# Two row maps for a subtract-mean-and-square kernel: runs of neighbouring partitions 64 KiB or 128 KiB apart

## The chip, the cores and the metric

The kernel runs on one core of one Trainium2 chip; nothing was launched on the other cores. Times are device microseconds (us) of a whole execution; the profile's span is shorter by some 1.8 us. The runs quoted here are in the fast state, except for four kernels that were looked at once each, whose state is unknown; the profiles report a granted clock of 1.000, and TensorE does no work. "Before" and "after" are the two kernels of the change.

HBM is the chip's main memory, SBUF the core's own memory of 128 partitions, and a DMA is a transfer between the two, shared out over 16 DMA engines. DVE, ACT, POOL and SP are the vector, scalar, GpSimd and sync engines; here SP issues the DMAs. A run is what one partition takes in one gapless piece of HBM, and the pitch is the distance between the starts of neighbouring partitions' runs. The trace records each transfer as packets, one for each run here (80 of the 720 in the two profiles are tiny ones of 4 bytes beside the data); sixteen packets started together, one on each engine, are called a batch. A transfer lands when its completion is seen.

## The reference, cut to what matters

```
x: (1024, 4096) float32, random normal; axis = -1
mean = np.mean(x, axis=axis, keepdims=True)
return ((x - mean) ** 2).astype(np.float32)
```

16.78 MB come in and 16.78 MB go out. Each row of 16 KiB needs its own mean and nothing from any other row, so which partition holds which row is free, as long as the output uses the same map as the input.

## The kernel before

Two tiles of 8.39 MB each lie in SBUF; a partition holds four rows of a tile (`Q = 4`), 64 KiB in one run of HBM. Tile 1 is loaded by two DMAs, a head of 512 columns and the rest; tile 2 by one; each tile is stored by one. All five go through one queue.

```python
Q = 4
HEAD = 512
H = D * 9 // 16                      # 2304 columns of row 2 on ACT, 1792 on DVE
ntiles = B // (P * Q)                # 2
x_t = x.rearrange("(n p q) d -> n p (q d)", p=P, q=Q)
out_t = out.rearrange("(n p q) d -> n p (q d)", p=P, q=Q)
# ... pools: one buffer per tile, so no load waits for a store ...
for i in range(ntiles):
    x_tile = io.tile([P, Q * D], F32)
    cuts = [0, HEAD, Q * D] if i == 0 else [0, Q * D]
    for lo, hi in zip(cuts, cuts[1:]):
        nc.sync.dma_start(out=x_tile[:, lo:hi], in_=x_t[i][:, lo:hi])
    tiles.append(x_tile)
# ... mean_on_act, mean_on_dve, square_on_act: one instruction or two on a row ...
for i in range(ntiles):
    row = [tiles[i][:, q * D:(q + 1) * D] for q in range(Q)]
    m3 = mean_on_act(row[3])
    m0 = mean_on_dve(row[0])
    square_on_act(row[3], m3)
    m1 = mean_on_dve(row[1])
    square_on_act(row[0], m0)
    m2 = mean_on_dve(row[2])
    square_on_act(row[1], m1)
    square_on_act(row[2][:, :H], m2)
    back = row[2][:, H:]
    nc.vector.tensor_scalar_add(out=back, in0=back, scalar1=m2)
    nc.vector.tensor_mul(out=back, in0=back, in1=back)
    nc.sync.dma_start(out=out_t[i], in_=tiles[i])
```

Of the kernel before, what the change touches and what calls it, by code (L numbers as in the profile page):

```python
# [2 lines left out]

os.environ.setdefault("NEURON_RT_ULTRASERVER_MODE", "4")

# [4 lines left out]

F32 = mybir.dt.float32
ACT = mybir.ActivationFunctionType


@with_exitstack
def kernel(
    ctx: ExitStack,
    tc: tile.TileContext,
    x: bass.AP,
    axis: bass.AP,  # L20
    out: bass.AP,
):




    nc = tc.nc

    B, D = x.shape
    P = nc.NUM_PARTITIONS  # L30
    Q = 4
    HEAD = 512
    H = D * 9 // 16
    assert B % (P * Q) == 0
    ntiles = B // (P * Q)
    inv_d = 1.0 / float(D)

    x_t = x.rearrange("(n p q) d -> n p (q d)", p=P, q=Q)
    out_t = out.rearrange("(n p q) d -> n p (q d)", p=P, q=Q)

    io = ctx.enter_context(tc.tile_pool(name="io", bufs=ntiles))
    scratch = ctx.enter_context(tc.tile_pool(name="scratch", bufs=1))
    stats = ctx.enter_context(tc.tile_pool(name="stats", bufs=2 * ntiles * Q))

    tiles = []
# [7 lines that stand above are left out]
    inorder = tc.keep_in_program_order  # L53

    def mean_on_act(row):
        copy = scratch.tile([P, D], F32)
        neg_mean = stats.tile([P, 1], F32)
        nc.scalar.activation(  # L58
            out=copy, in_=row, func=ACT.Identity, scale=-inv_d, accum_out=neg_mean
        )  # L60
        return neg_mean

    def mean_on_dve(row):
        neg_sum = stats.tile([P, 1], F32)
        neg_mean = stats.tile([P, 1], F32)
        inorder(nc.vector.reduce_sum(  # L66
            out=neg_sum, in_=row, axis=mybir.AxisListType.X, negate=True
        ))
        inorder(nc.vector.tensor_scalar_mul(out=neg_mean, in0=neg_sum, scalar1=inv_d))  # L69
        return neg_mean  # L70

    def square_on_act(part, neg_mean):
        inorder(nc.scalar.activation(  # L73
            out=part, in_=part, func=ACT.Square, bias=neg_mean, scale=1.0
# [18 lines that stand above are left out]
# [1 line left out]
_INS = ['x', 'axis']  # L94
_OUTS = [((1024, 4096), 'float32')]

_NUMBERS = {'axis': -1}


# [26 lines left out]
```

## Time and profile before

| | before |
|---|---|
| time, median of 3 runs | 83.02 us (83.0 to 83.2) |
| span of the profiled run | 81.2 us |
| DMA engines busy | 96.2% of 16 engines' span |
| DVE, ACT busy | 33.4 us, 34.7 us |

Two more views carry the argument besides those that the prediction shows. The first is the list of costliest groups (line, engine, operation, shapes and count; then busy us and mean ns of one; then the engine's idle time just before and what ended it).

```profile
L66 DVE TENSOR_REDUCE neg_sum<-x_tile 128x1 f32<-128x4096 f32 x6 | 26.5, 4413 | 24.9 <-DMA x_tile<-in_x_dram 24.9
...
L58 ACT ACTIVATE copy<-x_tile 128x4096 f32<-128x4096 f32 x2 | 7.2, 3616 | 23.0 <-DMA x_tile<-in_x_dram 23.0
L89 DVE TENSOR_TENSOR x_tile<-x_tile 128x1792 f32<-128x1792 f32 x2 | 4.1, 2026 | 0.1
L88 DVE TENSOR_SCALAR x_tile<-x_tile,neg_mean 128x1792 f32<-128x1792 f32 x2 | 2.3, 1153 | 0.1
```

The two groups with idle time before them wait for a load, 24.9 and 23.0 us; nothing else on DVE or ACT waits for more than fractions of a us. The second view is the DMA queue's own waits:

```profile
SPq L90 <- DVE x_tile L89: 54.7, 2, 35.9
SPq L121 <- DMA out_dram<-x_tile: 21.2, 2, 19.2
```

The queue's sequencer waits for compute before each store (54.7 us over two waits).

### The profile page before, as it was taken

The numbers are of one execution on the slowest core, as the hardware profiler recorded it, in microseconds if no ns is written. First come the engines' busy times: TensorE is split into PE (matmuls) and PEld (weight loads), VectorE is DVE, ScalarE is ACT, GpSimd is POOL, SyncE is SP. The second block draws the span as 40 slices with busy tenths as digits, with TensorE's granted clock in tenths as the row PEclk, the third lists the DMA queues.
The fourth block names the chain that finished last, engine by engine and source line by source line (L and its number), as shares of the span: only waits on it lengthen the run. The fifth ranks groups of instructions, "written<-read, shape, count | busy, mean of one in ns | idle before, by whom it ended". The sixth has DMA issues, their size and how long they took to land.

```text
span 81.2 us, 83 instructions
## 1 busy us (share of the span) xinstructions
DVE 33.4 (41%) x16; ACT 34.7 (43%) x13; POOL 0.2 (0%) x4
## 2 busy tenths in 40 slices
DVE  0000000000099999999349999999800000000000
ACT  6000000000099999999249999999800000000000
POOL 0000000000000000000000000000000000000000
DMA  1999569999974999990999990999992899997490
GB/s 16 614 501 501 219 282 501 501 501 501 517 323 194 517 517 517 517 484 32 517 517 517 517 517 0 517 517 517 517 517 129 388 517 517 517 517 323 194 517 0
DMA packets 720, 33.55 MB, mean 413 GB/s; under 512 B 80, under 2 KB 80, under 8 KB 208
## 3 DMA queue, kind: packets, MB, share of 16 engines
q1 hardware_dynamic: 720, 33.55, 96.2%
HBM read 16.78 MB, written 16.78 MB: 413 GB/s over the span
## 4 chain that ended last, share of the span: by engine, by line
DMA 49%; DVE 21%; SPq 1%; issue 0%
DMA x_tile<-in_x_dram 49%; DVE neg_sum L66 16%; DVE x_tile L89 2%; DVE x_tile L88 1%; SPq L50 1%; DVE neg_mean L69 1%
## 5 line engine op out<-in xcount | busy, mean ns | idle before, releaser
L66 DVE TENSOR_REDUCE neg_sum<-x_tile 128x1 f32<-128x4096 f32 x6 | 26.5, 4413 | 24.9 <-DMA x_tile<-in_x_dram 24.9
L73 ACT ACTIVATE x_tile<-x_tile,neg_mean 128x4096 f32<-128x4096 f32 (+1 forms) x8 | 26.0, 3324 | 0.1
L58 ACT ACTIVATE copy<-x_tile 128x4096 f32<-128x4096 f32 x2 | 7.2, 3616 | 23.0 <-DMA x_tile<-in_x_dram 23.0
L89 DVE TENSOR_TENSOR x_tile<-x_tile 128x1792 f32<-128x1792 f32 x2 | 4.1, 2026 | 0.1
L88 DVE TENSOR_SCALAR x_tile<-x_tile,neg_mean 128x1792 f32<-128x1792 f32 x2 | 2.3, 1153 | 0.1
L58 ACT ACT_TABLE_LOAD x1 | 1.3, 1283 | 0.7 <-PEq L107 0.7
L69 DVE TENSOR_SCALAR neg_mean<-neg_sum 128x1 f32<-128x1 f32 x6 | 0.9, 154 | 0.2
L58 ACT ACTIVATION_READ_ACCUMULATOR copy<-x_tile 128x1 f32 x2 | 0.4, 186 | 0.0
L107 POOL MEMSET const-bfloat16-1.0<- 128x1 bf16 x1 | 0.1, 103 | 0.0
L107 POOL MEMSET const-uint8-127<- 128x1 uint8 x1 | 0.1, 103 | 0.0
L107 POOL MEMSET const-float32-1.0<- 128x1 f32 x1 | 0.1, 100 | 0.0
L107 POOL MEMSET const-float32-0.0<- 128x1 f32 x1 | 0.1, 99 | 0.2 <-issue 0.2
## 6 DMA issues: line engine op xcount, KB each, us to landing
x_tile<-in_x_dram SPq DMA_DIRECT2D x1, 7936.0 KB, 21.2
x_tile<-in_x_dram SPq DMA_DIRECT2D x1, 256.0 KB, 2.7
out_dram<-x_tile SPq DMA_DIRECT2D x2, 21.7
x_tile<-in_x_dram SPq DMA_DIRECT2D x1, 40.1
```

The costliest lines, as they stand in the source:

```text
L50: nc.sync.dma_start(out=x_tile[:, lo:hi], in_=x_t[i][:, lo:hi])
L58: nc.scalar.activation(out=copy, in_=row, func=ACT.Identity, scale=-inv_d, accum_out=neg_mean)
L66: inorder(nc.vector.reduce_sum(out=neg_sum, in_=row, axis=mybir.AxisListType.X, negate=True))
L69: inorder(nc.vector.tensor_scalar_mul(out=neg_mean, in0=neg_sum, scalar1=inv_d))
L73: inorder(nc.scalar.activation(out=part, in_=part, func=ACT.Square, bias=neg_mean, scale=1.0))
L88: nc.vector.tensor_scalar_add(out=back, in0=back, scalar1=m2)
L89: nc.vector.tensor_mul(out=back, in0=back, in1=back)
L107: nc = _bacc.Bacc("TRN2", target_bir_lowering=False, num_devices=1)
```

## The change

Its intent: a partition owns eight consecutive rows of x, four in each tile, instead of four consecutive rows in each half of x. The runs of 64 KiB stay; the runs of neighbouring partitions in a tile are now 128 KiB apart instead of 64, and a tile is no longer one gapless piece of HBM. The head keeps its runs of 2 KiB.

```diff
-    x_t = x.rearrange("(n p q) d -> n p (q d)", p=P, q=Q)
-    out_t = out.rearrange("(n p q) d -> n p (q d)", p=P, q=Q)
+    x_t = x.rearrange("(p n q) d -> n p (q d)", p=P, q=Q)
+    out_t = out.rearrange("(p n q) d -> n p (q d)", p=P, q=Q)
```

An added blank line moves the line numbers by one: L66 of before is L67 of after.

## The prediction

> **What bounds the kernel now.** I read the page first, then the chain of waits, then the rate in each stretch between two landings. The first two lines below are the activity of the DMA engines, the next three the queue and the chain that ended last.
>
> ```profile
> DMA  1999569999974999990999990999992899997490
> GB/s 16 614 501 501 219 282 501 501 501 501 517 323 194 517 517 517 517 484 32 517 517 517 517 517 0 517 517 517 517 517 129 388 517 517 517 517 323 194 517 0
> ...
> q1 hardware_dynamic: 720, 33.55, 96.2%
> ...
> DMA 49%; DVE 21%; SPq 1%; issue 0%
> ```
>
> The DMA engines are busy for 96.2% of the span; DVE and ACT stand at 41% and 43%. The holes in the slice rows (219, 32, 0) are no pauses: a packet is put down to the slice in which it starts, one packet is a whole 64 KiB row, and all sixteen engines start theirs within about 0.3 us of each other. The trace's packet records settle it: 384 packets of 65,536 bytes, each 2.42 us, the next one starting on an engine when the last has ended. Slices of 2 us therefore see either one batch or none, and stretches have to be cut at the batches. Cut where one transfer hands over to the next (the columns are the stretch, its length, the busy time of DVE, ACT and POOL, the clock, the DMA share and the rate):
>
> ```profile
> 2.66:21.75 19.09, 0.00 (x0) 0.00 (x0) 0.00 (x0) 1.00 1.01 430
> 21.75:41.07 19.32, 16.71 (x8) 16.72 (x6) 0.00 (x0) 1.00 1.00 434
> 41.07:60.39 19.32, 16.71 (x8) 16.72 (x6) 0.00 (x0) 1.00 1.00 434
> 60.39:80.05 19.66, 0.00 (x0) 0.00 (x0) 0.00 (x0) 1.00 0.98 427
> ```
>
> These are load 1, load 2, store 1 and store 2, end to end. 8.39 MB in 19.32 us is 434 GB/s, the same for the load in row 2 and the store in row 3, and the DMA share is 1.00 in both. (The last window runs on a little past the last packet; at 19.32 us it ends at 79.7.) So the whole time is a sum: 2.66 us until the first large packet, 19.09, then 3 x 19.32 = 57.96, which makes 79.71; the last completion reaches the sequencer at 80.4, the teardown ends at 81.2, and the timed 83.02 is 1.8 above the span.
>
> The chain names DVE for 21% of the span, and I do not follow it. It goes from load 2 to the compute on tile 2, then stops at the last DVE instruction:
>
> ```profile
> 1.64 40.08 DMA x_tile<-in_x_dram
> ...
> 55.41 1.16 DVE x_tile L88
> ...
> 56.60 2.03 DVE x_tile L89
> ```
>
> Compute on tile 2 ends at 58.63. The second store is issued at 58.70 and its issue takes 0.34, so it is with the queue at 59.04. The first load was issued at 0.73 + 0.38 = 1.11 and its first packet started at 1.75, thus 0.64 from issue to packet; the store would be ready at about 59.7. But the engines are still on store 1 until 60.39. The compute has some 0.7 us of slack and is hidden, though not by much. The bound is the DMA rate alone.
>
> **What the Trainium skill says.** Three places bear on it. "DMA: Bandwidth & Descriptors", section Specifications, gives a ceiling of 435 GB/s for the sixteen engines; the trace agrees, 434. It means no placement in HBM can make the large transfers faster by more than a fraction of a per cent. The same page's section "Latency and other measured facts" has a row on the HBM row pitch at large powers of two: copies between HBM tensors in tiles of 128 partitions x 16 KiB ran at 207 GB/s in each direction at a pitch of 512 KiB per partition, 164 at 2 MiB, 103 at 4 MiB, against a full 214. This is the one statement that speaks of what the change touches; it calls its mechanism an inference. The kernel before has a pitch of 64 KiB and runs at the ceiling, which agrees with "no loss at small pitch" and shows nothing of larger ones. "HBM Reference", section Specifications, says that a core streaming alone measures well above its share of the domain, about 425 GB/s, bounded by its DMA engines; the trace agrees, since reading and writing show the same 434.
>
> **The change part by part.** It is two rearrange strings. Before, tile n, partition p held rows 512n + 4p to 512n + 4p + 3; now it holds rows 8p + 4n to 8p + 4n + 3. A partition still takes four whole rows, 64 KiB in one run, in each of two tiles. The mean is by row, so no result crosses a partition and the output goes back by the same map.
>
> Removed: nothing. Added: nothing. The instruction counts stay: 16 on DVE, 13 on ACT, five DMAs. So do all shapes: six reductions of 4.41 us, two scaled copies of 3.62, and the same squares. Compute stays 16.9 us per tile, from 41.74 to 58.63 for the second, beside the store of the first.
>
> Moved: HBM addresses. The start of partition p's run was at 64 KiB x p within a tile of 8 MiB without gaps; now it is at 128 KiB x p, with the other tile's runs in the gaps. The head of 512 columns is the first 2 KiB of each run: 128 packets of 2,048 bytes, before 64 KiB apart, now 128 KiB apart. The rest of tile 1 remains 128 packets of 63,488 bytes, and the other three transfers remain 128 packets of 65,536 bytes each, because a run is limited to 64 KiB by the partition's side of the transfer in either layout. That is 512 large packets, 32 on each engine, in both kernels. In time, per engine: 8 x 2.34 = 18.7 us and 24 x 2.42 = 58.1 us, nothing of it changed if a packet costs the same. The issue of a DMA is 0.34 to 0.43 us in rows where the HBM side is already strided (the head and the rest of tile 1: 0.38 and 0.43) and where it is contiguous (0.42 for load 2), so a strided description costs nothing more there.
>
> So the only term that can move is the packet time of 2.42 us. Each packet reads or writes 64 KiB in one sequence; the change alters which sixteen sequences run side by side. Working from the skill's row: its mildest bad pitch, 512 KiB, is four times ours and lost 3% (207 of 214). Ours at 128 KiB is nearer to the contiguous case, and its runs are four times longer. I estimate from that row a loss between 0 and 1% and put 0.1 us down for it: 83.02 + 0.1 gives 83.1.
>
> **The rivals.** First, **HBM aliasing already at 128 KiB.** For it: doubling a power-of-two step lets the sixteen simultaneous streams agree in one more address bit, and the engines start their packets within 0.3 us of each other. Against: 0.3 us is some 8 KiB of a stream's 64 KiB (0.3/2.42 of it), so they are spread; and the kernel before, with a power of two as well, shows not one slow packet in the last three transfers (2.418 to 2.432 us). If the full 3% of the 512 KiB case came in on all of the 77 us of transfers, the time would be 83.02 + 2.5 = 85.5, just into "slower". If only reads or only writes suffered it, half of that, 84.3, within 2%.
>
> Second, **the placement helps.** For it: the first batch of load 1 took up to 2.82 us instead of 2.34, and the 128 head packets, 0.08 us each when smooth, took up to 0.64; a different spacing could spread this start better. It would save at most about 0.5 us, giving 82.5, within 2%. Against: the head packets' delay looks like the latency of the first accesses[...]. Larger gains are barred by the ceiling that three transfers already run at.
>
> Third, **the wait of the second store becomes the bound.** It has 0.7 us of slack. If load 2 came later relative to store 1, the compute would follow and a hole open between the stores. But store 1 sits in the queue behind load 2 (issued at 39.42 while load 2 moves until 41.07), so a later load moves both by the same amount; only compute slower by over 0.7 us, or a store 1 that became shorter, would open it. Nothing here changes compute. I give it no share.
>
> Fourth, a **hidden transfer**: the head feeds nothing on its own, since compute waits for a whole row and starts at 22.4. If its 2 KiB packets became twice as slow (8 per engine x 0.08 = 0.7 us), it would delay all behind it by 0.7 us at most: 83.7, same.
>
> **Range and chances.** The three timed runs lie within 83.0 to 83.2. Around 83.1 I take 82.7 below (a small part of the second rival) and 84.0 above (1.2% loss of the transfers). Slower by over 2% needs 84.7, thus 1.7 us, or 2.2% of the 77 us of transfers, near the whole of the skill's 512 KiB loss at a quarter of that pitch: 0.07. Faster by over 2% needs 1.6 us less than a sum that already runs at the ceiling: 0.01. Same: 0.92.
>
> **What the profile after would show.** Right: 720 packets, 33.55 MB, a DMA share near 96%; load 2 and store 1 in stretches of 19.3 us at 434 GB/s; landings at 22.4, 41.7, 61.1 and 80.4; compute on tile 2 from 41.7 to 58.6; the same rows for DVE and ACT. The aliasing rival would show the stretches longer than 19.4 us with a rate under 430 while DMA share stays 1.00, in reads, writes or both. The start rival would show in the landing of load 1 alone. What would make me wrong: more packets than 720 (the strided description cut into shorter runs), a packet time that depends on the pitch, or a hole ahead of store 2.

## The result, and the profile after

| | before | after |
|---|---|---|
| time, median of 6 runs | 83.06 us (83.0 to 83.2) | 83.09 us (82.9 to 83.28) |
| span of the profiled run | 81.2 us | 81.4 us |
| ratio after to before | | 0.9999, 95% interval 0.9982 to 1.0016 |

A ratio is the mean time of one kernel's fast runs over the mean of the other's fast runs of the same rounds, so it is not quite the ratio of the medians.

The page after, in the parts that the prediction showed of before:

```profile
DMA  1999939999992999993899998399999199999290
GB/s 26 602 499 468 406 156 468 499 499 499 516 451 97 483 516 516 516 483 161 387 516 516 516 483 387 161 516 516 516 516 451 64 516 516 516 516 483 129 419 0
...
q1 hardware_dynamic: 720, 33.55, 95.9%
...
DMA 49%; DVE 21%; SPq 1%; issue 0%
```

Again 720 packets and 33.55 MB; the holes in the slice row sit in other slices, because they only mark where the engines' starts fall. Cut at this run's own hand-overs, the four transfers are as follows (stretch, length, busy time of DVE, ACT and POOL, clock, DMA share, GB/s):

```profile
2.66:21.50 18.84, 0.00 (x0) 0.00 (x0) 0.00 (x0) 1.00 1.02 434
21.50:41.03 19.53, 16.71 (x8) 16.72 (x6) 0.00 (x0) 1.00 0.99 430
41.03:60.35 19.32, 16.71 (x8) 16.72 (x6) 0.00 (x0) 1.00 1.00 434
60.35:79.67 19.32, 0.00 (x0) 0.00 (x0) 0.00 (x0) 1.00 1.00 434
```

Store 1 and store 2 take 19.32 us, as before (for store 2 of before, counted to the first engine's end as the prediction notes). The two loads share one small irregularity: the engine that comes first is done with load 1 earlier, 21.50 instead of 21.75, and one packet late in load 2 took 2.49 us. The packet records say the same in one number: the mean of the 384 packets of 64 KiB is 2.418 us before and 2.419 after.

One thing in the trace does differ. The sixteen engines start their packets of a batch within 0.29 us of each other at load 2 before, and within 0.69 us after. The load lands only after the last engine has ended (41.58 after, 41.38 before, each time 0.3 us before the landing), so load 2 lands at 41.88 instead of 41.72, and store 2 at 80.56 instead of 80.38. These 0.2 us are one profiled run against one; the six timed runs of each kernel spread over 0.2 to 0.4 us and their ratio shows nothing of it. Nor is the spread a property of the pitch: in the four traces below that keep the long runs and load tile 2 at 128 KiB it is 0.42, 0.55, 0.71 and 0.85 us at load 2.

### The profile page after: what moved, and what is told of

It reads as the page before. It is cut to its first block, busy times and chain, and to the rows that moved or that the text cites. A ratio compares the mean times of both kernels' runs of the same rounds, so it can differ in the third digit from the quotient of the medians.

```text
span 81.4 us, 83 instructions
## 1 busy us (share of the span) xinstructions
DVE 33.4 (41%) x16; ACT 34.7 (43%) x13; POOL 0.2 (0%) x4
## 2 busy tenths in 40 slices
DMA packets 720, 33.55 MB, mean 412 GB/s; under 512 B 80, under 2 KB 80, under 8 KB 208
## 3 DMA queue, kind: packets, MB, share of 16 engines
q1 hardware_dynamic: 720, 33.55, 95.9%
HBM read 16.78 MB, written 16.78 MB: 412 GB/s over the span
## 4 chain that ended last, share of the span: by engine, by line
DMA 49%; DVE 21%; SPq 1%; issue 0%
DMA x_tile<-in_x_dram 49%; DVE neg_sum L67 16%; DVE x_tile L90 2%; DVE x_tile L89 1%; SPq L51 1%; DVE neg_mean L70 1%
## 5 line engine op out<-in xcount | busy, mean ns | idle before, releaser
L67 DVE TENSOR_REDUCE neg_sum<-x_tile 128x1 f32<-128x4096 f32 x6 | 26.5, 4412 | 25.0 <-DMA x_tile<-in_x_dram 25.0
```

Source lines behind the costliest of these rows:

```text
L67: inorder(nc.vector.reduce_sum(out=neg_sum, in_=row, axis=mybir.AxisListType.X, negate=True))
```

## The experiments

A result of "nothing" needs more care than a gain: two effects may cancel, or the term that was touched may be off the path. **Theory:** the rate of the DMA engines sets the time, a 64 KiB packet costs 2.42 us at either pitch, and everything else is hidden. **Rivals:** the chain of waits with DVE in it is the bound after all; the pitch costs something that long runs or the head hide; the pitch never matters, at any size.

All kernels start from after unless said otherwise. The ratios are to the runs of before, since after was not run again; the result above has the two equal.

### Compute off and on the path

```diff
-        m2 = mean_on_dve(row[2])
+        m2 = m1  # wrong on purpose: one reduction fewer per tile
```

> The changed kernel with one of the three DVE reductions (4.4 us) left out in each tile; wrong on purpose. Theory (the DMA rate is the bound, compute is hidden with some 0.7 us of slack): 83.1, within 0.3. Rival (the chain of waits is the bound, with DVE's 21% of the span on it): the second tile's compute ends 4 us sooner, or as soon as ACT is done, and the time falls by up to 4 us, to about 79.

Measured: 83.14 us (82.92 to 83.34, 4 runs) beside 83.13 of before; ratio 0.9984, interval 0.9933 to 1.0034. (The comparison with the reference still passed it: the means of two random rows of 4096 are nearly alike.) The page:

```profile
DVE 24.5 (30%) x12; ACT 34.7 (43%) x13; POOL 0.2 (0%) x4
```

DVE does 8.9 us less (33.4 to 24.5) and the time does not move. This settles less than I had meant. ACT still works on tile 2 until 58.86, so store 2 is issued when it was issued before, as two lines of this trace show:

```profile
45.84 13.02 ACT L74 ACTIVATE x_tile<-x_tile,neg_mean 128x4096 f32<-128x4096 f32 x4
...
58.88 0.34 SPq L91 DMA_DIRECT2D out_dram<-x_tile  x1
```

and one of after:

```profile
58.85 0.34 SPq L91 DMA_DIRECT2D out_dram<-x_tile  x1
```

The compute of a tile did not become shorter; only one of two equally long engines did. The time would have stayed even if compute as a whole were the bound. It shows that less work on DVE alone gains nothing; whether compute is hidden is told by the next kernel.

```diff
-        square_on_act(row[2][:, :H], m2)
-        back = row[2][:, H:]
+        cut = H if i == 0 else D // 4
+        square_on_act(row[2][:, :cut], m2)
+        back = row[2][:, cut:]
```

> The changed kernel with 3072 instead of 1792 columns of row 2 of the second tile on DVE: the two DVE steps grow from 1.15 + 2.03 to about 1.98 + 3.47 us, 2.3 us more. Theory (0.7 us of slack): a hole of about 1.6 us opens ahead of store 2 and the time is 84.7 (84.3 to 85.0). Rival (much more slack than I read, or the store's start costs nothing): 83.1.

Measured: 84.25 us (84.04 to 84.46, 4 runs) beside 83.13; ratio 1.0109, interval 1.005 to 1.0168. The expected range began at 84.3, so the median lies just under it. Store 1, the hole and store 2, in the same columns as above:

```profile
41.09:60.41 19.32, 18.05 (x8) 15.66 (x6) 0.00 (x0) 1.00 1.00 434
60.41:61.98 1.57, 0.66 (x1) 0.00 (x0) 0.00 (x0) 1.00 0.01 0
61.98:81.30 19.32, 0.00 (x0) 0.00 (x0) 0.00 (x0) 1.00 1.01 434
```

The predicted hole is there: the engines end store 1 between 60.41 and 61.12, and none starts store 2 before 61.98. In the trace of after there is no such gap: the first engine ends store 1 and starts store 2 at 60.35. DVE's two last steps took 1.82 + 3.36 = 5.18 us instead of 1.15 + 2.03 = 3.18, so compute grew by 2.0 (not by the 2.3 I had scaled), and the time by 1.1. The difference, 0.9 us, is the slack that compute has before it costs anything. The interval of the ratio, 0.4 to 1.4 us of growth, leaves it anywhere between 0.6 and 1.6, so the 0.7 that I had read is not excluded, while a compute without slack, which would have cost 2.0, is. One thing was simplified in my reading: it took the first engine's hand-over. In this trace the last engine ends store 1 0.7 us after the first (61.12), and the landing waits for the last one, so part of the hole only takes up that stagger.

### The head

```diff
-        cuts = [0, HEAD, Q * D] if i == 0 else [0, Q * D]
+        cuts = [0, Q * D]
```

> The changed kernel without the head: tile 1 loaded in one transfer of 64 KiB runs. Theory (the head's 128 packets at 0.08 us cost what the shorter long packets save, and no compute waits for it): 83.0, within 0.3. Rival (the head's spacing of 128 KiB costs or hides something at the start): a change of 0.5 us or more, in the landing of load 1.

Measured: 83.29 us (83.09 to 83.35, 4 runs) beside 83.13; ratio 0.9998, interval 0.9949 to 1.0046 (one of the runs of before took 83.94 and widens it). Load 1 landed at 22.8 us; it did so at 22.5 in after and 22.4 in before. The head is worth nothing measurable here either way, within 0.4 us. Its own packets show the same of the doubled spacing: the 128 of 2 KiB took 0.12 us on the mean before and 0.11 after, and the head landed at 3.47 and 3.35.

### Shorter runs at both pitches

If runs of 64 KiB spread the engines enough to hide aliasing, shorter runs should bring it out. First, every transfer in runs of 16 KiB, one DMA per row, at the pitch of before and at that of after:

```diff
-        cuts = [0, HEAD, Q * D] if i == 0 else [0, Q * D]
+        cuts = [q * D for q in range(Q + 1)]
...
-        nc.sync.dma_start(out=out_t[i], in_=tiles[i])
+        for q in range(Q):
+            part = slice(q * D, (q + 1) * D)
+            nc.sync.dma_start(out=out_t[i][:, part], in_=tiles[i][:, part])
```

> The kernel before (pitch 64 KiB) with every transfer cut by rows: runs of 16 KiB, four DMAs a tile each way. Theory (engine rate is the bound at any run of 16 KiB or more): 83.1, within 0.6. Rival (short runs in step alias): slower than at 64 KiB runs.

> The changed kernel (pitch 128 KiB) with every transfer cut by rows: runs of 16 KiB. Theory: as the one at 64 KiB, within 0.3 us. Rival (the pitch matters, but runs of 64 KiB spread the streams and hide it): slower than the one at 64 KiB by over 1%.

Then the whole load of tile 1 in runs of 2 KiB, which makes 32 heads of it:

```diff
-        cuts = [0, HEAD, Q * D] if i == 0 else [0, Q * D]
+        cuts = list(range(0, Q * D + 1, HEAD)) if i == 0 else [0, Q * D]
```

> The kernel before (pitch 64 KiB) with the whole load of the first tile in runs of 2 KiB like the head: 32 DMAs of 512 columns. Theory: 256 packets on each engine at 0.084 us make 21.5 us instead of 19.4 for load 1; time about 85.3 (84.5 to 87, more if the 0.4 us of each issue shows).

> The changed kernel (pitch 128 KiB) with the whole load of the first tile in runs of 2 KiB: 32 DMAs of 512 columns. Theory (a packet costs the same at both pitches): the same as at 64 KiB, within 0.4 us. Rival (short runs at a power-of-two pitch run in step and alias): load 1 longer than at 64 KiB by over 0.5 us, median of the 2 KiB packets above 0.084.

All four ran on one chip, beside 83.08 us of before. Packet times are worked out from the traces' packet records.

| runs | pitch | time, median of 4 (range) | ratio to before | packet, median | packet, mean |
|---|---|---|---|---|---|
| 16 KiB everywhere | 64 KiB | 84.38 (84.32 to 84.45) | 1.0151 | 0.611 us | 0.623 us |
| 16 KiB everywhere | 128 KiB | 84.30 (84.22 to 84.41) | 1.0141 | 0.611 us | 0.623 us |
| 2 KiB in load 1 | 64 KiB | 87.07 (86.99 to 87.31) | 1.0479 | 0.084 us | 0.091 us |
| 2 KiB in load 1 | 128 KiB | 87.21 (86.62 to 87.53) | 1.0467 | 0.084 us | 0.091 us |

Between the two pitches there is no difference in either pair: 0.08 us the one way, 0.14 the other, both inside the runs' own spread. So long runs were not hiding a cost of the pitch between 64 and 128 KiB.

The level was missed in both pairs. I had expected 83.1 for runs of 16 KiB; it is 1.3 us more. Four packets of 0.611 are 2.444 us where one of 64 KiB takes 2.418; times 32 such groups on an engine this is 0.8 us. The other 0.5 lies in the last of the four DMAs of load 2, whose packets are slower in both traces (mean 0.70 us): it lands 5.4 us (64 KiB) and 5.65 us (128 KiB) after the one before it, where the six before it came every 4.9. Why it is slow stays open. "Slower than with runs of 64 KiB" was also what the rival of the first of these runs had said; that both pitches pay alike, with the median at 0.611 in both, speaks for a cost of cutting and against the pitch, but a loss that is equal at both pitches is not excluded. For 2 KiB I had expected 85.3: 256 packets on an engine at the mean of 0.091 instead of the median 0.084 make 1.8 us more, which is the miss.

### The pitch made much larger

x holds 16.78 MB, so 128 KiB x 128 partitions is the largest pitch that fits it. For more, the second tile is stored to a scratch tensor of wider rows (2 MiB each) of which only the first 64 KiB are used; wrong, since half of the output is never written.

```diff
+    wide = nc.dram_tensor("wide", (P, 2048 * 256), F32, kind="Internal").ap()
...
-        nc.sync.dma_start(out=out_t[i], in_=tiles[i])
+        to = out_t[i] if i == 0 else wide[:, :Q * D]
+        nc.sync.dma_start(out=to, in_=tiles[i])
```

> The changed kernel with the second tile stored to a scratch tensor at a pitch of 2 MiB per partition instead of 128 KiB; wrong on purpose. Theory A (128 KiB is free because it is small; the loss that the skill gives for 2 MiB, 164 against 214, applies): store 2 takes about 25 us instead of 19.3 and the time is about 89. Theory B (one direction of 64 KiB runs never notices the pitch, the engines' own rate is the limit): 83.1, packets still 2.42 us.

Measured: 88.86 us (88.77 to 89.26, 4 runs) beside 83.13; ratio 1.068, interval 1.0624 to 1.0736. Theory A had said about 89. Load 2, store 1 at 128 KiB and store 2 at 2 MiB, in one trace:

```profile
21.60:40.96 19.36, 16.71 (x8) 16.73 (x6) 0.00 (x0) 1.00 0.99 430
40.96:60.28 19.32, 16.71 (x8) 16.73 (x6) 0.00 (x0) 1.00 1.01 438
60.28:85.34 25.06, 0.00 (x0) 0.00 (x0) 0.00 (x0) 1.00 0.97 332
```

The same bytes in the same 128 packets take 25.06 us instead of 19.32, with the DMA engines nearly as busy (the last window runs on to the last engine's end; to the first engine's end, as in the other rows, it is 24.0). The packets grew, from 2.42 to 3.04 us on the mean. Theory B, that the pitch never matters, falls. A loss at a large pitch is real on this chip, then, and 128 KiB is too little to call it up. The reason that the prediction weighed, streams that run in step, is not shown: the store's first batch, started within 0.51 us, still took 2.42 us a packet, and the second, started within the same 0.51 us, took 3.00. Note that the busy share tells nothing of this: 95.9% in after, 95.5% here.

Where does it begin, and do loads suffer too? In four more kernels tile 1 is stored raw to the scratch tensor and tile 2 is loaded from there (wrong on purpose, one look each, state unknown; the last of the four ran on another chip than the other three); the pitch of the scratch tensor is 128 KiB, 512 KiB, 1 MiB or 2 MiB.

```diff
+    wide = nc.dram_tensor("wide", (P, 512 * 256), F32, kind="Internal").ap()   # 128, 512, 1024, 2048
...
+        if i == 1:
+            nc.sync.dma_start(out=wide[:, :Q * D], in_=tiles[0])
+        source = x_t[0] if i == 0 else wide
         for lo, hi in zip(cuts, cuts[1:]):
-            nc.sync.dma_start(out=x_tile[:, lo:hi], in_=x_t[i][:, lo:hi])
+            nc.sync.dma_start(out=x_tile[:, lo:hi], in_=source[:, lo:hi])
```

> The changed kernel with tile 1 stored raw to a scratch tensor at a pitch of 512 KiB and tile 2 loaded from there; wrong on purpose: a pitched store and a pitched load in one trace beside an ordinary load and two stores at 128 KiB. Theory (loss grows with the pitch, as the skill's row has it, 207 of 214): the pitched store and load take about 20 us each instead of 19.3, packets 2.42 to 2.50; whole time about 105 (five transfers of 19.3, plus two waits of some 2 us for a landing). Rival (runs of 64 KiB hide any aliasing below 2 MiB): packets 2.42 in both.

> The same at a pitch of 1 MiB. Theory (loss grows gradually between 512 KiB and 2 MiB): packets between 2.5 and 2.9 us in the pitched store, load likewise. Rival (a step: free up to 1 MiB, all of the loss at 2 MiB): 2.42.

> The same at a pitch of 2 MiB. Theory (the loss is of the addresses, whatever the direction): the pitched store's packets at 3.04 us on the mean as in the run before, and the pitched load's too; whole time about 116. Rival (a store's loss only, since a load can run ahead): the load's packets stay at 2.42 and the time is about 110.

The first of these left an ambiguity: at 512 KiB the store was as quick as ever and the load was not. So the control at 128 KiB followed:

> The same detour through a scratch tensor at a pitch of 128 KiB, as a control for the three wider ones: it tells the pitch from the detour itself (a load that starts on idle engines and reads what was just written). Theory (the 23.7 us that the load took from issue to landing at 512 KiB were the pitch): here the load takes about 21 us, as the store did, packets near 2.42 on the mean; whole time about 105.3. Rival (the detour's load is slow at any pitch): 23.7 us again, packets near 2.67, about 108.

From the chain of waits of each trace (start us, length us, what), the store and the load through the scratch tensor. At 128 KiB:

```profile
22.94 20.72 DMA wide<-x_tile
...
43.68 22.99 DMA x_tile<-wide
```

At 512 KiB:

```profile
22.47 20.73 DMA wide<-x_tile
...
43.21 23.74 DMA x_tile<-wide
```

At 1 MiB:

```profile
22.68 26.90 DMA wide<-x_tile
...
49.60 26.58 DMA x_tile<-wide
```

At 2 MiB:

```profile
22.69 26.86 DMA wide<-x_tile
...
49.57 26.26 DMA x_tile<-wide
```

These lengths run from issue to landing, so they hold 1.2 to 1.7 us more than the packets of the store. A load of 128 packets is eight batches of sixteen; its first batch starts on idle engines and its last is followed by a store. The table has the means of the packets, with the load's six middle batches by themselves.

| pitch of the scratch tensor | time (one run) | store: packet mean | load: packet mean | load: middle six batches |
|---|---|---|---|---|
| 128 KiB | 107.87 us | 2.43 us | 2.64 us | 2.42 us |
| 512 KiB | 108.16 us | 2.43 us | 2.67 us | 2.42 us |
| 1 MiB | 117.38 us | 3.08 us | 2.75 us | 2.69 us |
| 2 MiB | 117.03 us | 3.06 us | 2.89 us | 2.76 us |

Read with the control, 512 KiB costs nothing: the store's packets are at 2.43 in both, and the load's slowness stands at 128 KiB too, in its first and last batches alone; why these two are slow, at any pitch, stays open. My theory for that run had blamed the pitch for part of it, and the control's rival, "the detour's load is slow at any pitch", took the point. Between 512 KiB and 1 MiB there is a step: the store's packets go from 2.43 to 3.08 us, and 2 MiB adds nothing to that. Both expectations for the store at 1 MiB were wrong, the gradual one (2.5 to 2.9) as well as the step at 2 MiB (2.42); the load there, 2.75 on the mean, fell into the gradual range. Loads suffer as well, but less: 11% and 14% in the middle batches (2.69 and 2.76 over 2.42), where the stores lose 27% and 26% over all their batches, and 34% and 30% in their middle six (3.24 and 3.15). At 2 MiB the store came as expected (3.04); neither expectation for the load (3.04, or 2.42) was right.

Why loads lose less, and what makes the step, stays open. The first batch of both slow stores starts within 0.15 us and takes 2.46 us, as in the control; the later, slower ones start 0.16 to 1.26 us apart. So how far apart the engines start does not tell a slow batch from a quick one. Two rivals were left untested. The scratch tensor grows with its pitch (16, 64, 128 and 256 MiB), so its sheer extent, or where it lies in HBM, is not parted from the pitch. And every pitch here is a power of two: no padded one was run, so "large" is not parted from "large power of two".

No version came out of this that beats the two kernels: from load 2 on the transfers run back to back at 430 to 434 GB/s in both, and no kernel here was quicker beyond the noise.

## Why the prediction was right

**The bound.** Right. The transfers end to end make the time; after shows the same stretches at the same rate. The prediction's refusal to follow the chain into DVE holds: 2.0 us more compute at the end cost 1.1, and store 2 follows store 1 without a gap in both kernels. The 8.9 us taken off DVE show less than that, since ACT took as long as before.

**The parts of the change.** Right. Nothing was added, removed or cut up: 720 packets in both, and the predicted landings of 22.4, 41.7, 61.1 and 80.4 came at 22.5, 41.9, 61.3 and 80.6 in the profiled run. The allowance of 0.1 us for the pitch cannot be told from zero: the medians differ by 0.03 and the interval of the ratio reaches from -0.15 to +0.13 us.

**Aliasing at 128 KiB.** Rightly put low, but the reasons given for it did not hold up. The prediction scaled down from a loss of 3% at 512 KiB, as if the loss shrank with the pitch; here there is none even at 512 KiB with these runs (one run), and the loss comes as a step after it, at a pitch eight times that of the change. The estimate of 0 to 1% was safe on either shape, so its coming true does not bear out the scaling. The argument that the spread of the engines within a run protects the long runs fails too: runs of 16 KiB and 2 KiB are indifferent to the two pitches as well, and at 2 MiB the packets of 64 KiB grew to 3.04 us although the engines started 0.5 to 1.1 us apart, more than the 0.3 that was to protect them.

**The placement helps at the start.** It did not. The long packets of load 1 still begin 2.67 us into the span in both kernels, and the slowest of its first batch took 2.99 us after, 2.82 before (one trace each).

**Store 2's wait.** The mechanism was right: more compute opened the hole. Its slack of 0.7 us is within what the run leaves (0.6 to 1.6; 0.9 by the medians).

**The head.** Right as far as tested: without it the time is the same within half a per cent.

## What to carry to other kernels

When the DMA engines are busy back to back at their full rate, ask of a change in layout only whether a packet will take longer; packet counts and sizes answer most of it, and a pitch of 64 to 512 KiB between partitions did not matter here, in either direction. At 1 and 2 MiB the packets of a store took about a quarter more time, with a nearly unchanged busy share, so judge DMA by GB/s in a stretch and not by the share. Do not take an engine in the chain of waits for the bound before you have checked whether the transfer that it releases could have started any sooner.

## What the Trainium skill lacked or had wrong

- "DMA: Bandwidth & Descriptors", section "Latency and other measured facts", the row on the HBM row pitch: it has no figure below 512 KiB and none at 1 MiB. Here 64 and 128 KiB are equal (ratio 0.9999) at runs of 64, 16 and 2 KiB (the shorter ones in their own pairs), and 1 MiB is already as bad for a store as 2 MiB (packets of 3.08 and 3.06 us against 2.43, one run each).
- The same row gives 207 of 214 GB/s at 512 KiB, for copies within HBM in runs of 16 KiB. Transfers between HBM and SBUF in runs of 64 KiB lost nothing at 512 KiB here (2.43 us a packet in the store, as at 128 KiB). At 2 MiB its 164 of 214, a factor of 0.77, fits our store (2.42 over 3.04 is 0.80) but not our load (2.42 over 2.76 in its middle batches is 0.88); the row does not tell the two directions apart.
- "HBM Reference", section Specifications (TRN2), says about 425 GB/s for a core streaming alone; here the stretches run at 434, reading and writing, 2% more. The prediction called that agreement.
- No page has a measured cost for cutting a long transfer into runs of 16 KiB: it is 1.4 to 1.5% of the whole time here, of which packets of 0.611 us (four for 2.444, against 2.418 for one of 64 KiB) are the larger part.
